# Keeping the two parts of mem in a DRAM scratch tensor between its four uses

## The chip, the cores and the metric

The kernel runs on one core of a Trainium2 chip. The metric is the device time of one execution in microseconds. The times quoted are medians of several runs; one further execution was recorded by the hardware profiler, and all rows of the trace come from it.

The engines appear under the names that the profile uses: PE (TensorE matmul), PEld (its weight loads), DVE (VectorE), ACT (ScalarE), POOL (GpSimd) and SP (SyncE, which issues most of the DMAs here).

## What is computed

A two-layer encoder trunk over 512 rows of width 1024. Each layer has a mixer, a cross-attention into `mem` (256 rows of width 1024, the same in both layers) and a gated MLP with a width-3 convolution; after each of the three the rows are normalised:

```python
for layer in range(DEPTH):                      # DEPTH = 2
    mix = mixer_ab(x, ...) if layer % 2 == 0 else mixer_c(x, ...)
    x = layer_norm(alpha * x + mix, ...)
    x = layer_norm(alpha * x + cross_attend(x, mem, wq, wkv, wo), ...)
    x = layer_norm(alpha * x + conv_ffn(x, w_up, conv_w, conv_b, w_down), ...)

def cross_attend(x, mem, wq, wkv, wo):
    kv = mem @ wkv                              # keys and values, 4 heads of 256
    probs = softmax(q @ k.T * 256 ** -0.5)
    return (probs @ v) @ wo
```

`mem` itself never changes, so the kernel reads the same 1 MB four times: for the keys and for the values of each layer.

## The kernel before

**Numbers in two parts.** Every fp32 operand x of a matmul is split into a high part h (x rounded to the fp32r type) and a low part l = x - h. `split` (lines 85 and 86) does it: a cast on ACT writes h, then a subtraction on DVE writes l. `mm3` (lines 223 to 225) makes a product of three matmuls: h h, h l, l h. In the trace a matmul row reads `ps<-moving,stationary`; weights are called `wh` and `wl`, activations `act`, accumulators in PSUM `ps`.

**Weights.** `plan` (from line 111) lists all weight tiles in the order of use. `Weights.load` keeps up to four of them loaded ahead: the DMA goes out on SP into one of 7 buffers `raw` (128x1024, 512 KB), and later `split` moves it into one of 5 pairs `wh`, `wl`. A `raw` buffer is free again when DVE has subtracted, a `wh` buffer when PE has used it. SP issues its DMAs in program order, so a DMA that has to wait for its buffer holds up all that follow.

**Activations.** 12 slots `act` of 128x2048 (h in the left half, l in the right). `mem`, turned so that its features lie on the partitions, takes two of them at each use: `load_mem` (line 639) calls `load_split` for each half, that is a 512 KB DMA into a `raw` buffer (line 90), a cast and a subtraction (128x1024 each).

**The four uses of mem.** First: loaded while the mixer's output projection of layer 0 runs, used by `proj_k` of layer 0. Second: loaded in `attend` of layer 0 after the queries, used by `proj_v` of layer 0. Third: loaded in the last down-projection of the MLP of layer 0, used by `proj_k` of layer 1. Fourth: loaded in the output projection of the mixer of layer 1, used by `proj_v` of layer 1. For the first, third and fourth the call comes through `ahead` from `load_ahead` (line 807).

**The fast product.** The third and fourth load stand in `fast_product` (lines 367 to 464), a product with seven block multiplications in place of eight. It goes through the weights in four passes. The passes use sums of weights that POOL makes: for each weight row of the second pass, lines 166 to 168 compute t3 (into a buffer `row`), t2 (in place, in the `raw` buffer of one weight, reading t3 and the second weight) and t4. So the second pass needs both weights of a row on chip before its first cast. The accumulators X and Y run on from the first pass into the second, and X into the third; between the passes DVE adds them to the rows x (line 379), and PE may go on in X only when DVE has read it. `ahead` is called inside the second pass.

**Order.** Each engine works through its own list in order. The order in the lists is made by a scheduler when the kernel is built, from the program order and estimated times, so leaving out instructions can also move others.

Of the kernel before, what the change touches and what calls it, by code (L numbers as in the profile page):

```python
# [8 lines left out]
F32 = mybir.dt.float32  # L9
# [5 lines left out]
P = 128  # L15
# [10 lines left out]
CH = 1024  # L26
# [10 lines left out]
def kernel(ctx: ExitStack, tc: tile.TileContext, a: dict, out: bass.AP):  # L37
    nc = tc.nc
# [8 lines left out]
    tpool = ctx.enter_context(tc.tile_pool(name="tpool", bufs=4))  # L47
    fpool = ctx.enter_context(tc.tile_pool(name="fpool", bufs=1))
    spool = ctx.enter_context(tc.tile_pool(name="spool", bufs=4))
    pspool = ctx.enter_context(tc.tile_pool(name="pspool", bufs=8, space=PSUM))  # L50

    uid = [0]

    def nm(s):
        uid[0] += 1
        return f"{s}{uid[0]}"
# [7 lines left out]
    def slot(dtype=F32R):  # L64

        return apool.tile([P, 2 * CH], dtype, tag="act", name=nm("act"))

    def duo(tag="act"):
        if tag == "act":
            t = slot()  # L70
            return t[:, :CH], t[:, CH:]
        h = wpool.tile([P, CH], F32R, tag="wh", name=nm("wh"))
        l = wpool.tile([P, CH], F32R, tag="wl", name=nm("wl"))
        return h, l

    def raw_tile():
        return rpool.tile([P, CH], F32, tag="raw", name=nm("raw"))
# [5 lines left out]
    def split(h, l, src):  # L83

        nc.scalar.copy(h, src)  # L85
        nc.vector.tensor_sub(l, src, h.bitcast(F32))  # L86

    def load_split(src, tag):
        raw = raw_tile()
        nc.sync.dma_start(raw, src)  # L90
        h, l = duo(tag)
        split(h, l, raw)
        return h, l
# [542 lines left out]
        return y  # L636


    def load_mem():
        return [load_split(a["memT"][i], "act") for i in range(2)]  # L640

    def mem_at(t, i, k, c):
        return t[k // 4][i][:, (k % 4) * MEM + c.start : (k % 4) * MEM + c.stop]
# [37 lines left out]
    def attend(layer, xT, kT, v):  # L681
# [55 lines left out]
        if v is None:  # L737
            for m in range(8):
                queries(m, m + 1)
            o, v, mem = Act(8), {}, load_mem()  # L740
            scores(0)
            v[0] = proj_v(layer, mem, 0)
            turn(0)
            scores(1)
            values(0)
            v[1] = proj_v(layer, mem, 1)
            turn(1)
            scores(2)
            values(1)
        else:  # L750
            for m in range(6):
                queries(m, m + 1)
            scores(0)
            queries(6, 7)
            scores(1)
            queries(7, 8)
            o = Act(8)
            turn(0)
            scores(2)
            turn(1)  # L760
            values(0)
            values(1)
# [39 lines left out]
        weights.load_beside(2 if k < 2 else 1, a["xT"][k], xT.tiles[k])  # L802
    weights.done(RING - 4)

    mem, left = [], None

    def load_ahead():
        mem.append(load_mem())

    for layer in range(2):  # L810
        if layer == 0:
            y = mixer_ab(xT)
            xT, left = residual_norm([(lambda: y, 0, 8)], "ab_w_out", "ln_mix", layer, ahead=load_ahead)
            kT = proj_k(layer, mem.pop(), {2: left[0]})
            v = None
        else:
            kT = proj_k(layer, mem.pop(), dict(zip((1, 2, 3), left)))
            y = mixer_c(xT)
            xT, left = residual_norm([(lambda: y, 0, 8)], "c_w_out", "ln_mix", layer, ahead=load_ahead)
            v = {0: proj_v(layer, mem[0], 0, {2: left[0]}), 1: proj_v(layer, mem.pop(), 1, {0: left[1], 5: left[2]})}  # L820
        o, hooks = attend(layer, xT, kT, v)
        xT, left = residual_norm([(lambda: o, 0, 8)], "xa_wo", "ln_xa", layer, hooks=hooks)
        up = [(lambda m0=m0, m1=m1, xT=xT, late=left[0]: ffn_up(layer, xT, late, m0, m1), m0, m1) for m0, m1 in FFN_GROUPS[layer]]
        xT, left = residual_norm(up, "ffn_w_down", "ln_ffn", layer, layer == 1, ahead=None if layer else load_ahead)
# [57 lines left out]
def build(shapes):  # L882
    import concourse.bacc as bacc

    nc = bacc.Bacc("TRN2", target_bir_lowering=False, num_devices=1)
    aps = {n: nc.dram_tensor(f"in_{n}", s, F32, kind="ExternalInput").ap() for n, s in shapes.items()}
    out = nc.dram_tensor("out_0_dram", (1, S, D), F32, kind="ExternalOutput").ap()
    with tile.TileContext(nc) as tc:
        kernel(tc, aps, out)
    return nc  # L890
# [9 lines left out]
```

## Time and profile before

| | us |
|---|---|
| Median of three runs | 1338.54 |
| The three runs | 1338.54, 1337.86, 1340.98 |
| The profiled execution | 1340.83 |
| Its span (first to last instruction) | 1339.1 |
| DVE busy | 880.7 |
| ACT busy | 511.2 |
| POOL busy | 190.3 |
| Mean granted clock of TensorE | 0.996 of full speed |

The profiled execution's time is 1.7 us longer than its span. "Busy" is the sum of the durations of an engine's instructions; issuing DMAs does not count. Matmuls are pipelined, with starts 0.23 us apart in a stream of 128x512 ones though each row is 0.39 us long, so time that PE loses is best seen in the distance between two starts. `[1.21 <-DVE wl L86]` behind a row is idle time of that engine just before it, and what ended it.

### The profile page before, as it was taken

The page shows a single profiled execution, that of the slowest core. Times are in us where ns is not written, and L with a number is a line of the kernel's source. Part 1 is how long each engine was busy: PE and PEld are TensorE (multiplying, and loading weights), DVE is VectorE, ACT ScalarE, POOL GpSimd, SP SyncE. Part 2 cuts the span into 40 slices and gives each one's busy share as a digit, 9 for nine tenths or more (in the row PEclk, how much of TensorE's full clock was granted, in tenths as well). Part 3 has the DMA queues.
Part 4 walks back from the last instruction along what each step waited for, and adds up shares of the span by engine and source line. Part 5 has one row for each costly group of instructions (what it writes and reads, how often), then busy time and mean ns, then how long its engine had stood idle before and what let it go on. Part 6 is the DMA issues. An engine that isn't in the chain of part 4 may idle for free.

```text
span 1339.1 us, 16258 instructions
## 1 busy us (share of the span) xinstructions
PE 1322.8 (99%) x6397; PEld 1113.0 (83%) x6397; DVE 880.7 (66%) x1135; ACT 511.2 (38%) x659; POOL 190.3 (14%) x160
## 2 busy tenths in 40 slices
PE   9999999999999999999999999999999999999996
PEld 7888888898888888887988887788898888888885
DVE  6668446576675676578945569936676685577446
ACT  5342344324343434343433334434144343343330
POOL 1002000010340220142100142100001320141001
PEclk9999999999999999999999999999999999999998
DMA  8633534223344344237433237531132353236301
GB/s 319 210 123 103 170 124 126 63 64 105 107 167 131 98 144 140 87 102 243 160 101 95 87 115 239 188 95 48 48 111 87 118 180 118 79 123 223 94 1 63
DMA packets 49469, 167.37 MB, mean 125 GB/s; under 512 B 5872, under 2 KB 6000, under 8 KB 49392
## 3 DMA queue, kind: packets, MB, share of 16 engines
q1 hardware_dynamic: 47664, 160.03, 36.9%
q0 software_dynamic: 1728, 6.29, 1.4%
q8 instruction: 50, 0.82, 0.2%
q14 instruction: 27, 0.22, 0.1%
HBM read 164.21 MB, written 2.10 MB: 124 GB/s over the span
## 4 chain that ended last, share of the span: by engine, by line
PE 92%; DVE 5%; issue 1%; DMA 1%; ACT 0%; POOL 0%; POOLq 0%; DVEq 0%; ACTq 0%
PE ps L223 30%; PE ps L224 30%; PE ps L225 30%; DVE wl L86 2%; PE ps L363 1%; DVE act L86 1%; DMA raw<-in_memT 1%; DVE x L338 1%; PE ps L724 1%; DVE stats L496 0%; DVE x L379 0%; POOL rs L335 0%; PE ps L798 0%; DVE x L336 0%; PE ps L598 0%
## 5 line engine op out<-in xcount | busy, mean ns | idle before, releaser
L86 DVE TENSOR_TENSOR wl<-raw,wh 128x1024 fp32r<-128x1024 f32 (+1 forms) x275 | 344.6, 1259 | 267.0 <-ACT wh L85 259.7
L85 ACT CAST wh<-raw 128x1024 fp32r<-128x1024 f32 (+1 forms) x275 | 286.5, 1042 | 540.1 <-PE ps L224 310.5
L223 PE MATMUL ps<-act,wh 128*128 128x512 f32 (+1 forms) x1284 | 472.6, 368 | 0.5 <-DVE act L86 0.5
L224 PE MATMUL ps<-act,wh 128*128 128x512 f32 (+1 forms) x1284 | 472.5, 368 | 0.0
L225 PE MATMUL ps<-act,wl 128*128 128x512 f32 (+1 forms) x1284 | 472.3, 368 | 0.0
L223 PEld LDWEIGHTS ps<-act,wh 128*128 128x128 f32 x1284 | 242.0, 189 | 41.1 <-DVE act L86 0.9
L224 PEld LDWEIGHTS ps<-act,wh 128*128 128x128 f32 x1284 | 242.1, 189 | 40.3 <-DVE act L86 0.3
L225 PEld LDWEIGHTS ps<-act,wl 128*128 128x128 f32 x1284 | 242.1, 189 | 40.2
L223 PE MATMUL ps<-wh,act 128*128 128x512 f32 (+1 forms) x664 | 259.6, 392 | 1.5 <-DVE x L379 1.5
L224 PE MATMUL ps<-wl,act 128*128 128x512 f32 (+1 forms) x664 | 258.7, 390 | 2.2 <-DVE wl L86 2.2
L225 PE MATMUL ps<-wh,act 128*128 128x512 f32 (+1 forms) x664 | 258.1, 389 | 0.0
L224 PEld LDWEIGHTS ps<-wl,act 128*128 128x128 f32 x664 | 125.2, 189 | 29.6 <-DVE wl L86 4.6
L223 PEld LDWEIGHTS ps<-wh,act 128*128 128x128 f32 x664 | 125.6, 189 | 28.8 <-DVE x L379 3.1
L225 PEld LDWEIGHTS ps<-wh,act 128*128 128x128 f32 x664 | 125.2, 189 | 25.6
L335 POOL TENSOR_TENSOR rs<-rs,mhalf 128x1 f32<-128x1 f32 x28 | 41.0, 1468 | 535.4 <-DVE rs L334 508.5
L159 POOL TENSOR_TENSOR raw<-raw,raw 128x512 f32<-128x512 f32 x23 | 32.6, 1415 | 449.7 <-DVE wl L86 375.1
L85 ACT CAST act<-ps 128x512 fp32r<-128x512 f32 x104 | 56.8, 591 | 71.1 <-PE ps L363 51.9
L86 DVE TENSOR_TENSOR act<-ps,act 128x512 fp32r<-128x512 f32 x104 | 67.5, 683 | 10.9 <-ACT act L85 10.8
L379 DVE SCALAR_TENSOR_TENSOR x<-x,ps 128x512 f32<-128x512 f32 x96 | 61.6, 679 | 9.8 <-PE ps L225 9.8
L86 DVE TENSOR_TENSOR act<-blocks,act 128x768 fp32r<-128x768 f32 (+1 forms) x46 | 61.5, 1349 | 8.5 <-ACT act L85 8.5
L625 DVE SCALAR_TENSOR_TENSOR tmp<-ps,convw,tmp 128x511 f32<-128x511 f32 x88 | 65.6, 745 | 1.6
L784 DVE TENSOR_TENSOR blocks<-tmp,ps 128x512 f32<-128x512 f32 x38 | 26.1, 687 | 59.8 <-PE ps L225 57.6
(80 smaller groups left out, 810.1 us busy)
## 6 DMA issues: line engine op xcount, KB each, us to landing
raw<-in_ffn_w_up SPq DMA_DIRECT2D x88, 512.0 KB, 3.6
raw<-in_ffn_w_down SPq DMA_DIRECT2D x63, 512.0 KB, 3.6
raw<-in_c_w_in SPq DMA_DIRECT2D x24, 512.0 KB, 3.6
raw<-in_xa_wk SPq DMA_DIRECT2D x16, 512.0 KB, 3.9
raw<-in_xa_wq SPq DMA_DIRECT2D x16, 512.0 KB, 4.1
raw<-in_xa_wv SPq DMA_DIRECT2D x16, 512.0 KB, 3.6
raw<-in_xa_wo SPq DMA_DIRECT2D x16, 512.0 KB, 4.2
raw<-in_c_w_out SPq DMA_DIRECT2D x12, 512.0 KB, 3.6
```

The costliest lines, as they stand in the source:

```text
L85: nc.scalar.copy(h, src)
L86: nc.vector.tensor_sub(l, src, h.bitcast(F32))
L159: nc.gpsimd.tensor_sub(both("t1"), w1[:, half[0]], w0[:, half[0]])
L223: nc.tensor.matmul(ps, lh, rh, start=start, stop=False, skip_group_check=more)
L224: nc.tensor.matmul(ps, lh, rl, start=False, stop=False, skip_group_check=more)
L225: nc.tensor.matmul(ps, ll, rh, start=False, stop=stop, skip_group_check=more)
L335: nc.gpsimd.tensor_tensor(rs, rs, mhalf, op=ALU.pow)
L338: nc.vector.scalar_tensor_tensor(z[:, c], z[:, c], rs[:, 0:1], b[:, c], op0=ALU.mult, op1=ALU.add)
L363: nc.tensor.transpose(ps[:, k * P : (k + 1) * P], xt[t][:, (half * 4 + k) * P : (half * 4 + k + 1) * P], ident)
L379: return nc.vector.scalar_tensor_tensor(z, z, scale, ps, op0=ALU.mult, op1=ALU.add)
L625: nc.vector.scalar_tensor_tensor(dst[:, s:], src[:, : S - s], tap(2 - s), dst[:, s:], op0=ALU.mult, op1=ALU.add)
L784: hid.put(m, lambda to: nc.vector.tensor_mul(to, *(v.rearrange("p (i s) -> p i s", i=2) for v in (g, ps[2 * i + 1]))))
```

## The change

A pool in DRAM with two tensors `mem0` and `mem1` (128x2048, 1 MB each) is added. The first call of `load_mem` does what it did, and stores each slot, h and l side by side, to its tensor. The other three calls load the slots from these tensors: one 1 MB DMA for each half, no `raw` buffer, no cast and no subtraction. All of these DMAs are issued on SP.

```diff
+    dpool = ctx.enter_context(tc.tile_pool(name="dpool", bufs=1, space=bass.MemoryType.DRAM))
...
-    def load_mem():
-        return [load_split(a["memT"][i], "act") for i in range(2)]
+    memory = [dpool.tile([P, 2 * CH], F32, tag=f"mem{i}", name=f"mem{i}") for i in range(2)]
+
+    def load_mem(first=False):
+
+        tiles = []
+        for i in range(2):
+            t = slot()
+            tiles.append((t[:, :CH], t[:, CH:]))
+            if first:
+                raw = raw_tile()
+                nc.sync.dma_start(raw, a["memT"][i])
+                split(*tiles[i], raw)
+                nc.sync.dma_start(memory[i], t.bitcast(F32))
+            else:
+                nc.sync.dma_start(t.bitcast(F32), memory[i])
+        return tiles
...
-    mem, left = [], None
+    mem, left, first = [], None, [False, False, True]
 
     def load_ahead():
-        mem.append(load_mem())
+        mem.append(load_mem(first.pop()))
```

Lines of the kernel after the change stand one lower up to line 639, and buffers have other numbers: what is `x_113` to `x_116` before is `x_115` to `x_118` after. The accumulators X, Y of the product named below are `ps_4779`, `ps_4780` (X) and `ps_4781`, `ps_4782` (Y) in both.

**SP at the third use** (end of the last down-projection of layer 0). Before:

```order
L147 DMA raw_4834<-in_ffn_w_down 128x1024
L147 DMA raw_4836<-in_ffn_w_down 128x1024
L90 DMA raw_4919<-in_memT 128x1024
L90 DMA raw_4924<-in_memT 128x1024
L183 DMA raw_4929<-in_xa_wk 128x1024
L183 DMA raw_4947<-in_xa_wk 128x1024
```

After:

```order
L148 DMA raw_4834<-in_ffn_w_down 128x1024
L654 DMA act_4919<-mem_119 128x2048
L148 DMA raw_4836<-in_ffn_w_down 128x1024
L654 DMA act_4921<-mem_120 128x2048
L184 DMA raw_4923<-in_xa_wk 128x1024
L184 DMA raw_4941<-in_xa_wk 128x1024
```

The first load of mem has moved ahead of `raw_4836`, the second weight that POOL needs for the last row of the second pass, and is twice as large. The fourth use has the same pattern with `in_c_w_out`.

**DVE at the third use**, between the second and the third pass. `wl_4932` and `wl_4950` are weights of the third and the fourth pass, `wl_4968` the last of the fourth. Before:

```order
L496 BN_STATS stats_4776<-x_114 128x6
L86 TENSOR_TENSOR act_4921<-raw_4919,act_4921 128x1024
L86 TENSOR_TENSOR act_4926<-raw_4924,act_4926 128x1024
L86 TENSOR_TENSOR wl_4932<-row_4807,wh_4931 128x1024
L86 TENSOR_TENSOR wl_4950<-raw_4718,wh_4949 128x1024
L86 TENSOR_TENSOR wl_4968<-raw_4810,wh_4967 128x1024
L379 SCALAR_TENSOR_TENSOR x_113<-x_113,ps_4779 128x512
L379 SCALAR_TENSOR_TENSOR x_114<-x_114,ps_4780 128x512
```

After (`wl_4926`, `wl_4944` and `wl_4962` are the same three weights):

```order
L497 BN_STATS stats_4776<-x_116 128x6
L87 TENSOR_TENSOR wl_4926<-row_4807,wh_4925 128x1024
L87 TENSOR_TENSOR wl_4944<-raw_4718,wh_4943 128x1024
L380 SCALAR_TENSOR_TENSOR x_115<-x_115,ps_4779 128x512
L87 TENSOR_TENSOR wl_4962<-raw_4810,wh_4961 128x1024
L380 SCALAR_TENSOR_TENSOR x_116<-x_116,ps_4780 128x512
```

The two subtractions of mem are gone, and the addition from the first accumulator stands ahead of the last weight's subtraction.

**PE at the third use**, from the end of the second pass. Before:

```order
L225 MATMUL ps_4782<-wh_4893,act_4772 128x512
L223 MATMUL ps_4905<-wh_4949,act_4309 128x512
L224 MATMUL ps_4905<-wl_4950,act_4309 128x512
L225 MATMUL ps_4905<-wh_4949,act_4309 128x512
L223 MATMUL ps_4906<-wh_4949,act_4309 128x512
L223 MATMUL ps_4779<-wh_4897,act_4309 128x512
L224 MATMUL ps_4779<-wl_4898,act_4309 128x512
```

After:

```order
L226 MATMUL ps_4782<-wh_4893,act_4772 128x512
L224 MATMUL ps_4779<-wh_4897,act_4309 128x512
L225 MATMUL ps_4779<-wl_4898,act_4309 128x512
L226 MATMUL ps_4779<-wh_4897,act_4309 128x512
L224 MATMUL ps_4780<-wh_4897,act_4309 128x512
```

Four matmuls of the fourth pass (into `ps_4905` and `ps_4906`) stood ahead of the third pass and now follow it, so that the third pass, with `ps_4779`, comes directly behind the second. The fourth use has both of these shifts too.

At the first use each store to `mem0`, `mem1` stands on SP behind the subtraction of its half, with four and two of the loads of `xa_wk` of layer 0 after them. At the second use the two loads stand behind the first two loads of `xa_wo` instead of ahead of them.

## The prediction

> **What bounds the kernel now.** I read the page's busy line first, then PE's waits, then the two stretches in which PE waits, there the chain and the timelines.
>
> The busy line of the page:
>
> ```profile
> PE 1322.8 (99%) x6397; PEld 1113.0 (83%) x6397; DVE 880.7 (66%) x1135; ACT 511.2 (38%) x659; POOL 190.3 (14%) x160
> ```
>
> PE is busy for 1322.8 of 1339.1 us. Work taken off DVE and ACT can therefore be worth only what PE waits for them. All of PE's waits but one at the start (engine, line, awaited: total us, times, longest):
>
> ```profile
> PE ps L224 <- DVE wl L86: 2.2, 2, 1.2
> PE ps L223 <- DVE x L379: 1.5, 2, 0.8
> PE ps L363 <- DVE act L86: 0.7, 1, 0.7
> PE ps L223 <- DVE act L86: 0.5, 2, 0.3
> ```
>
> That is 4.9 us, all on DVE. The windows view (length, then busy us of PE, PEld, DVE, ACT, POOL, granted clock, DMA share, GB/s) shows where:
>
> ```profile
> 621.00:629.00 8.00, 6.01 (x18) 4.17 (x18) 7.56 (x11) 1.04 (x1) 0.53 (x1) 0.79 0.98 342
> 629.00:665.00 36.00, 35.25 (x261) 33.28 (x261) 34.74 (x47) 17.97 (x24) 6.09 (x4) 1.00 0.47 153
> 821.00:826.00 5.00, 3.22 (x13) 2.06 (x12) 5.00 (x6) 1.04 (x1) 0.53 (x1) 1.00 0.86 265
> 826.00:865.00 39.00, 38.49 (x184) 31.24 (x182) 38.44 (x53) 18.98 (x24) 8.29 (x6) 1.00 0.60 208
> ```
>
> Place A is 621 to 629 (third use of mem), place B 821 to 826 (fourth). Both are the last quarter of a fast product, and DVE is nearly full there and after. At A the clock is 0.79 over 8 us, that is 0.21 x 8 = 1.7 us of PE time lost, beside the waits. The first and second use (near 90 and 190 us) lie in stretches without a wait.
>
> The chain of work at A (start, us, what):
>
> ```profile
> 605.68 5.57 DMA raw<-in_memT
> ...
> 612.23 1.05 ACT wh L85
> ...
> 613.31 0.99 DVE wl L86
> ...
> 618.06 1.86 DVE act L86 x2
> ...
> 620.24 3.49 DVE wl L86 x3
> 623.73 0.61 DVE x L379
> ```
>
> So mem is in it twice: ACT, in order, stands before the two casts of mem until its load lands, and the weight cast behind them starts at 612.23; then the two splits on DVE (the 1.86 of the chain) stand ahead of the weight splits and of the addition that PE waits for. PE and DVE there:
>
> ```profile
> 621.05 0.39 PE L223 MATMUL ps<-wh,act 128*128 128x512 f32 x1
> 622.65 0.50 PE L224 MATMUL ps<-wl,act 128*128 128x512 f32 x1 [1.21 <-DVE wl L86]
> 622.99 0.40 PE L225 MATMUL ps<-wh,act 128*128 128x512 f32 x1
> 623.22 0.39 PE L223 MATMUL ps<-wh,act 128*128 128x512 f32 x1
> 624.38 0.58 PE L223 MATMUL ps<-wh,act 128*128 128x512 f32 x1 [0.77 <-DVE x L379]
> ```
>
> ```profile
> 617.98 2.35 DVE L86 TENSOR_TENSOR act<-raw,act 128x1024 fp32r<-128x1024 f32 x2
> ```
>
> From 622.99 to 623.22 the pitch of a matmul is 0.23. Against it the steps 621.05 to 622.65, 622.65 to 622.99 and 623.22 to 624.38 are 1.37 + 0.11 + 0.93 = 2.4 us too long. **A costs 2.4 + 1.7 = 4.1 us.** At B:
>
> ```profile
> 821.68 0.39 PE L223 MATMUL ps<-wh,act 128*128 128x512 f32 x1
> 823.07 0.50 PE L224 MATMUL ps<-wl,act 128*128 128x512 f32 x1 [1.01 <-DVE wl L86]
> 823.41 0.40 PE L225 MATMUL ps<-wh,act 128*128 128x512 f32 x1
> 823.65 0.39 PE L223 MATMUL ps<-wh,act 128*128 128x512 f32 x1
> 824.81 0.50 PE L223 MATMUL ps<-wh,act 128*128 128x512 f32 x1 [0.77 <-DVE x L379]
> ```
>
> 1.16 + 0.11 + 0.93 = **2.2 us at B**, at full clock.
>
> **The change part by part.** *Removed:* six casts on ACT and six splits on DVE, two at each later use. Those at the second use are worth nothing (no wait of PE near it). At A and B the two splits free 2.26 us of DVE (617.98 to 620.24), and the orders show that the additions from the first two accumulators now stand before or between the weight splits, and that PE no longer puts four products of the last weight ahead.
>
> *Place A worked through.* The big load goes onto SP's queue between the two last down-projection weights. Those two, the two loads of mem that now follow them, and the DMA traffic:
>
> ```profile
> L147 SPq DMA_DIRECT2D raw<-in_ffn_w_down x2: 327/327/327, 602.3 to 603.4; - x2
> ...
> DMA to landing us min/median/max: 3.5/4.2/4.9
> ```
>
> ```profile
> L90 SPq DMA_DIRECT2D raw<-in_memT x2: 328/328/328, 604.6 to 605.7; - x2
> ...
> DMA to landing us min/median/max: 5.4/5.5/5.6
> ```
>
> ```profile
> 608.00:610.00 2.00, 2.00 (x11) 1.65 (x10) 2.00 (x4) 0.02 (x1) 1.52 (x1) 1.00 0.90 367
> ```
>
> The first lands at 605.8, the second at 603.4 + 4.9 = 608.3. A megabyte at 367 GB/s takes 2.9 us, half a megabyte 1.4. With the big load ahead of it the second weight lands at 605.8 + 2.9 + 1.4 = 610.1, **1.8 us later**. POOL and ACT behind it:
>
> ```profile
> 608.42 1.52 POOL L167 TENSOR_TENSOR raw<-row,raw 128x512 f32<-128x512 f32 x1 [1.20 <-DMA raw<-in_ffn_w_down]
> ```
>
> ```profile
> 615.80 1.06 ACT L85 CAST wh<-raw 128x1024 fp32r<-128x1024 f32 x1 [0.63 <-PE ps L225]
> 618.57 1.05 ACT L85 CAST wh<-raw 128x1024 fp32r<-128x1024 f32 x1 [1.71 <-PE ps L225]
> ```
>
> L167 then runs 610.1 to 611.5. The cast that stood behind mem (612.23) can start at 611.5 and ends at 612.5, its split on DVE at 613.7 (a split takes 1.13 of DVE, an addition or a statistic 0.6), the first row weight's at 614.8, two additions and two statistics at 617.2, the second row weight's at 618.3, the next weight's at 619.5 (its cast, the 615.80 one, is long done), the addition from the first accumulator at 620.1, the last weight's split at 621.3 (cast 618.57), the addition from the second accumulator at 621.9. PE needs the first at 621.05 and the second three matmuls later, at 621.7. So the wait left is 0.2 us, and with it goes the half clock. **A gives 4.1 - 0.2 = 3.9.** What is late next is that second addition.
>
> *Place B:* the same order, with the two last weights of that product here:
>
> ```profile
> L147 SPq DMA_DIRECT2D raw<-in_c_w_out x2: 328/328/328, 801.0 to 804.1; - x2
> ```
>
> The second goes out 3.1 us after the first, so the big load is through before it: at most 0.6 us later. The wait left is 0.1: **2.1.**
>
> *The waits behind A and B* (36.00 - 35.25 = 0.75 and 39.00 - 38.49 = 0.51) are on transposes of normalised rows, with DVE full. At A DVE saves 2.26 of work, 0.8 by the earlier cast, and up to 1.3 of idle time that I put down to PE's slow stretch (34.74 of 36.00 busy): 4.3 against PE's 3.9. The wait stays or shrinks: 0.1. At B 2.26 + 0.8, the same earlier cast assumed, is 3.1 against 2.1: I take all of the 0.51. Together 0.6, with bounds of -1.0 (DVE does not follow) and +1.3.
>
> *Added at the first use:* two stores, each behind its split in SP's order, with the weights for the keys behind them. Second split of mem, and the next weight cast that needs a load from there:
>
> ```profile
> 96.26 1.22 DVE L86 TENSOR_TENSOR act<-raw,act 128x1024 fp32r<-128x1024 f32 x1
> ...
> 118.06 1.05 ACT L85 CAST wh<-raw 128x1024 fp32r<-128x1024 f32 x1 [4.83 <-PE ps L225]
> ```
>
> The last store waits until 97.5, the loads behind it land before 110, which is 8 us ahead of that cast: cost 0, and without that margin whatever passes 118. No store of this size is in the trace. Bounds: 0 and, as four of the slowest loads in a row (4 x 5.6 = 22 us from 97.5), 2 us. I take 0.
>
> *Second use:* the loads now stand behind two weights:
>
> ```profile
> L90 SPq DMA_DIRECT2D raw<-in_memT x2: 327/328/328, 177.1 to 182.6; - x2
> ```
>
> ```profile
> 194.01 0.40 PE L223 MATMUL ps<-wh,act 128*128 128x512 f32 x1
> ```
>
> Those weights take the two raw buffers and times of mem (177.1, 182.6); the first big load goes out at 183.0 and lands near 183 + 3.6 + 2.9 = 189.5, the first product of it is at 194.0. Cost 0, 4.5 us of cover; a load that took 11.2 us (two of 5.6) would land at 194.2: cost 0.2 at most.
>
> **Sum**, against the profiled execution (1340.83 us, span 1339.1): 3.9 + 2.1 + 0.6 = 6.6, so 1334.2. That execution stands 2.3 above the median of 1338.54, and the half-clock stretch may be its own: without it the gain is 4.9 and the median gives 1333.6. Between them, **1333.8 us**.
>
> [...]
>
> **The rivals.**
>
> *DVE takes the gain back at the transposes.* For it: 34.74 of 36.00 and 38.44 of 39.00 busy. Then A gives only what DVE saves itself, 2.26 + 0.8 = 3.1 of the profiled 4.1, less the 1.7 of clock where a run has none of it, and B 2.1 with no 0.6: about 3.4 off the median, 1335.1. Against it: the 1.3 of idle time. Chance 0.22.
>
> *The big load holds up the weights.* If a megabyte takes 5.6 us of the queue and not 2.9, the weight at A lands at 612.8, the whole chain above moves by 2.7, PE waits 1.75 for the first addition and 1.1 for the second: A's waits are as long as now, and B keeps 1.5: 1337.0. For it: DMA share 0.90 there. Against it: 367 GB/s. Chance 0.16. [...]
>
> *Slower.* The same mechanism past its point: from a landing of 613 on, each further us at A is a us of PE, beside the half clock. At 11.2 us a megabyte (two loads of 5.6 in a row) the weight lands at 618.4 and PE waits some 8 us at A for the 4.1 there now, as well as at B: up to 1348; halfway 1343. Chance 0.05.
>
> *The half clock was in every timed run:* 1338.54 - 6.6 = 1331.9. For it: the third timed run is 1340.98. Chance 0.12. *The reloading does not take place* (flag taken from the wrong end): the list ends in True, so the first load splits and three reload; 0.01, 1338.5.
>
> **How the numbers follow.** Forecast 0.44, at 1333.6 to 1334.2. A change of 0.3% (4.0 us, below 1334.5) is about what can be told from none. Faster: 0.12, nearly all of 0.44, a little of the first rival: 0.57. Same: the rest of the first two rivals and the last: 0.38. Slower 0.05. The range, 1331.5 to 1337.5, takes in the bounds of the waits behind A and B and most of the second rival.
>
> **What would show it.** PE's waits on DVE wl and x at A and B gone or under 0.3 us; clock 1.00 at A; POOL L167 starting near 610 there; no split act<-raw on DVE after 100 us. Wrong, if POOL L167 starts after 612.5, if PE waits more for transposes than the 0.75 and 0.51 now, or if PE waits near 194 us.

## The result and the profile after

The changed kernel takes **1332.08 us** (median of 4 runs, 1331.86 to 1332.91), the kernel before 1338.2 us beside it: ratio 0.995, 95% interval 0.9938 to 0.9962. The profiled execution took 1331.86 us with a span of 1330.1, 9.0 us less than the span before. The kernel before spreads more than the changed one: 1337.37 to 1345.07 in 18 later runs.

The busy line of the changed kernel, and all of PE's waits (engine, line, awaited: total us, times, longest). The helpers stand one line further down, so L223 of before is L224 here.

```profile
PE 1318.7 (99%) x6397; PEld 1111.3 (84%) x6397; DVE 873.0 (66%) x1129; ACT 505.9 (38%) x653; POOL 188.7 (14%) x160
```

```profile
PE ps L813 <- DVE zeros L810: 1.2, 1, 1.2
PE ps L225 <- DVE wl L87: 0.2, 1, 0.2
```

Of the 4.9 us of waits on DVE 0.2 is left, and that lies near 384 us, at neither place. The windows that answer to those of before (length, busy us of PE, PEld, DVE, ACT, POOL, granted clock, DMA share, GB/s):

```profile
617.00:625.00 8.00, 8.00 (x37) 6.47 (x36) 6.92 (x10) 3.16 (x3) 0.53 (x1) 1.00 0.87 279
625.00:661.00 36.00, 36.00 (x266) 34.11 (x265) 35.76 (x49) 17.41 (x23) 6.09 (x4) 1.00 0.48 159
809.00:817.00 8.00, 8.00 (x37) 6.46 (x36) 7.54 (x11) 3.01 (x4) 1.13 (x2) 1.00 0.89 341
817.00:856.00 39.00, 38.97 (x187) 32.10 (x187) 38.46 (x53) 19.62 (x25) 8.30 (x6) 1.00 0.59 197
```

PE has no idle time at A and behind it and 0.03 us behind B, the clock at A is 1.00 instead of 0.79 (half, 0.50, from 625 to 628 in the profile of before), and DVE is still nearly full behind both places (35.76 of 36.00, 38.46 of 39.00).

Where the 9.0 us came from is read from five matmuls that both programs run at the same point: one well ahead of A, one ahead of and one behind the transposes that follow A, one behind B, and one behind the waits that follow B. Before:

```profile
402.36 0.45 PE L223 MATMUL ps<-wh,act 128*128 128x512 f32 x1
649.28 0.36 PE L223 MATMUL ps<-act,wh 128*128 128x256 f32 x1
658.00 0.39 PE L223 MATMUL ps<-act,wh 128*128 128x256 f32 x1
847.47 0.48 PE L223 MATMUL ps<-wh,act 128*128 128x512 f32 x1
911.94 0.36 PE L223 MATMUL ps<-act,act 128*128 128x256 f32 x1
```

And after:

```profile
402.25 0.46 PE L224 MATMUL ps<-wh,act 128*128 128x512 f32 x1
644.88 0.36 PE L224 MATMUL ps<-act,wh 128*128 128x256 f32 x1
652.65 0.39 PE L224 MATMUL ps<-act,wh 128*128 128x256 f32 x1
839.86 0.48 PE L224 MATMUL ps<-wh,act 128*128 128x512 f32 x1
903.38 0.36 PE L224 MATMUL ps<-act,act 128*128 128x256 f32 x1
```

The lead is 0.11, 4.40, 5.35, 7.61 and 8.56 us. So A gave 4.3 (1.7 of it the half clock), the transposes behind A 0.95, B 2.26, the products behind B 0.95, and all the rest 0.5.

### The profile page after: what moved, and what is told of

It reads as the page before. It is cut to its first block, busy times and chain, and to the rows that moved or that the text cites. A ratio compares the mean times of both kernels' runs of the same rounds, so it can differ in the third digit from the quotient of the medians.

```text
span 1330.1 us, 16252 instructions
## 1 busy us (share of the span) xinstructions
PE 1318.7 (99%) x6397; PEld 1111.3 (84%) x6397; DVE 873.0 (66%) x1129; ACT 505.9 (38%) x653; POOL 188.7 (14%) x160
## 4 chain that ended last, share of the span: by engine, by line
PE 97%; DVE 1%; issue 1%; DMA 0%; POOL 0%; POOLq 0%; SPq 0%; DVEq 0%; ACT 0%
PE ps L225 32%; PE ps L224 32%; PE ps L226 32%; PE ps L364 1%; PE ps L739 1%; DMA raw<-in_ab_w_v 0%; POOL rs L336 0%; DVE x L339 0%; PE ps L599 0%; DVE wl L87 0%; DVE stats L497 0%; DVE act L87 0%; DVE x L489 0%; DVE blocks L275 0%; POOLq L903 0%
## 5 line engine op out<-in xcount | busy, mean ns | idle before, releaser
L87 DVE TENSOR_TENSOR wl<-raw,wh 128x1024 fp32r<-128x1024 f32 (+1 forms) x275 | 341.1, 1245 | 263.9 <-ACT wh L86 256.4
L224 PE MATMUL ps<-act,wh 128*128 128x512 f32 (+1 forms) x1284 | 472.2, 368 | 0.0
L224 PEld LDWEIGHTS ps<-act,wh 128*128 128x128 f32 x1284 | 242.0, 189 | 40.3 <-issue 0.3
L224 PE MATMUL ps<-wh,act 128*128 128x512 f32 (+1 forms) x664 | 258.1, 389 | 0.0
L224 PEld LDWEIGHTS ps<-wh,act 128*128 128x128 f32 x664 | 124.6, 188 | 26.6 <-DVE x L380 1.1
```

The lines of the kernel that those rows point to most:

```text
L224: nc.tensor.matmul(ps, lh, rh, start=start, stop=False, skip_group_check=more)
```

## The experiments

Each kernel computes the whole result. The first group is written against the changed kernel, whose `load_mem` has a mode there instead of the flag: "store" (split the input and store the parts), "split" (as before the change), "load" (from the scratch tensor) and three more that are shown where they are used.

**Which use gives what.** One kernel takes the second use back, one keeps the reload at the third use alone, one at the fourth alone, and one only stores.

```diff
 # second_split
-            o, v, mem = Act(8), {}, load_mem()
+            o, v, mem = Act(8), {}, load_mem("split")
 # only_third (the list is read from its end; the second use splits as well)
+    modes = ["split", "load", "store"]
 # only_fourth
+    modes = ["load", "split", "store"]
 # store_alone
+    modes = ["split", "split", "store"]
```

> The second use of mem casts and splits it from the input again, as the kernel before does; the first use splits and stores, the third and fourth load from the scratch tensor. It computes the whole result. Theory (the gain comes from the third use, A, and the fourth, B, alone): 1332.1 us, within 0.5, and no wait of PE near 190 us. Rival (the second use helps too, because its raw buffers or its place on SP come free for other weights): 1333 us or more, and loads or casts between 180 and 200 us that end later than in the changed kernel.

> Only the third use (A) loads the parts; the second and fourth split as before, the first splits and stores. It computes the whole result. Theory: PE's waits at A and on the transposes behind it go (2.4 + 0.75 = 3.2 us without the half-clock stretch, 4.9 with it), those at B stay at 2.2 and 0.5: 1335.0 us when the stretch is not in the timed runs, 1333.3 when it is. Rival (DVE is full behind A and gives the gain back at the transposes): 1336 us or more, with more than 0.75 us of waits on the transposes behind A.

> Only the fourth use (B) loads the parts; the second and third split as before, the first splits and stores. It computes the whole result. Theory: the waits at B (2.2 us) and on the transposes behind it (0.5 to 1.0) go, those at A stay: 1335.0 to 1335.5 us, and the gains of this kernel and of the one with only the third use add up to the 6.1 us of the whole change. Rival (DVE gives it back at the transposes behind B): 1336.2 us or more. If the half-clock stretch at A is in the timed runs, this kernel keeps it and stands 4.9 us above the changed one, at 1337.

> The first use splits and stores both halves; the other three uses split again as before and nothing reads the scratch tensor. It computes the whole result. Theory: the stores cost nothing, 1338.2 us within 0.5, with PE's waits at A and B as before (2.2 us on wl and 1.5 on x together). Rival (the stores or their places on SP hold up the weights of the keys): up to 1340.2 us, with a wait of PE before 130 us.

Measured beside 1339.07 us for the kernel before: second use split 1332.03 (ratio 0.9945, interval 0.9933 to 0.9958), third alone 1334.98 (0.9967, 0.9955 to 0.998), fourth alone 1335.47 (0.9973, 0.9962 to 0.9983), stores alone 1339.21 (0.9996, 0.9985 to 1.0007). The second use and the stores are worth nothing that can be measured. The two gains, 4.1 and 3.6, add up to 7.7, beside 7.0 for both in the same runs and 6.1 in the first. In the windows of the kernel with the third use alone, A is full and B still waits:

```profile
617.00:625.00 8.00, 8.00 (x37) 6.46 (x36) 7.89 (x12) 2.91 (x3) 0.53 (x1) 1.00 0.97 337
817.00:825.00 8.00, 5.96 (x26) 4.25 (x25) 8.00 (x12) 2.10 (x2) 0.53 (x1) 1.00 0.92 320
```

**Half of the split at a time.** At A and B one half of each part is loaded, the other made from the input as before.

```diff
 # keep_sub: the high half is loaded, ACT's cast is gone
+    nc.sync.dma_start(tiles[i][0].bitcast(F32), memory[i][:, :CH])
+    nc.vector.tensor_sub(tiles[i][1], raw, tiles[i][0].bitcast(F32))
 # keep_cast: the low half is loaded, DVE's subtraction is gone
+    nc.sync.dma_start(tiles[i][1].bitcast(F32), memory[i][:, CH:])
+    nc.scalar.copy(tiles[i][0], raw)
```

> At A and B the high half is loaded from the scratch tensor, and the low half is made on DVE by the subtraction from the input, as before; only the casts on ACT are gone. Second use loads. It computes the whole result. Theory (the two subtractions on DVE, ahead of the additions that PE waits for, are what costs): 2.26 us of DVE come back at each place; about 1.0 of it fits in DVE's idle time there, so PE waits 1.3 at each place and a little behind it: 1334.7 to 1335.5 us. Rival (the casts on ACT, in order behind the landing of mem, are what costs): 1332.1 to 1332.6 us, no wait at A or B.

> At A and B the low half is loaded from the scratch tensor, and the high half is cast on ACT from the input, as before; only the subtractions on DVE are gone. Second use loads. It computes the whole result. Theory (DVE's subtractions are what costs, the casts delay the next weight cast by 0.8 us only): 1332.1 to 1332.9 us, waits at A and B together under 0.8 us. Rival (the casts on ACT are what costs): 1335 to 1337.5 us, with waits on wl at A and B near 1 us each.

Both missed what either theory gave: keep_sub 1348.68 us beside 1338.86 (1.0068, 1.0054 to 1.0082), slower than before by 9 to 10, and keep_cast 1339.27 (0.9998, 0.9986 to 1.0009; its runs lie between 1335.92 and 1342.2). The first of keep_sub's subtractions on DVE, and the matmul that then waits at A (idle time ahead of a row and what ended it in brackets):

```profile
611.16 1.23 DVE L655 TENSOR_TENSOR act<-raw,act 128x1024 fp32r<-128x1024 f32 x1 [5.10 <-DMA raw<-in_memT]
```

```profile
615.34 0.76 PE L224 MATMUL ps<-wh,act 128*128 128x512 f32 x1 [4.62 <-DVE x L380]
```

The scheduler had put the subtraction early on DVE, ahead of a weight split. The two loaded halves go ahead of the inputs on SP, 2 MB with them, and DVE, in order, stood 5.1 us before a load. In keep_cast the same happens to ACT, where the last row is the weight cast:

```profile
610.91 1.05 ACT L659 CAST act<-raw 128x1024 fp32r<-128x1024 f32 x1 [3.38 <-DMA raw<-in_memT]
612.16 1.05 ACT L659 CAST act<-raw 128x1024 fp32r<-128x1024 f32 x1 [0.20 <-DMA raw<-in_memT]
613.12 1.04 ACT L86 CAST wh<-raw 128x1024 fp32r<-128x1024 f32 x1
```

That cast is at 609.69 in the changed kernel. So these two tested the landing of the input more than the work. What they show is the price of an engine that stands, in its order, before a load that has not landed: 5.1 and 3.38 us here.

**More bytes.** Each reload is issued twice.

```diff
+            elif mode == "twice":
+                for _ in range(2):
+                    nc.sync.dma_start(t.bitcast(F32), memory[i])
```

> At A and B each half of mem is loaded from the scratch tensor twice into the same buffer; the second copies stand behind the first on SP and wait for these to land, with the weights of the next product behind them (2 MB more at each place). Second use loads once. It computes the whole result. Theory (the reloads have some 9 us of room: the first weight behind them lands near 612 and its cast is at 621): that weight lands near 618.5, so 1332.1 to 1333 us and no wait at A or B over 0.5 us. Rival (the queue is the bound there, and transfers that come later stop PE): 1335 us or more, PE waiting for weights behind A and B.

Measured 1333.05 us (0.995, 0.9938 to 0.9963), as the theory had it. SP's queue at A shows the first weight of the next product some 8 us later than in the changed kernel (604.24):

```profile
612.81 11.32 SPq L184 DMA_DIRECT2D raw<-in_xa_wk  x8
```

Two more megabytes at each place cost about 1 us in all. They stand behind the weights that A itself waits for, and PE has no wait at A or B. How much could be put ahead of those was not tried.

**The clock.** The kernel before once more, for another profile.

> The kernel before, unchanged, for another profile of it. Theory: the waits of PE at A and B come back at 2.2 and 1.5 us in total, but the half-clock stretch at A is a matter of the single execution: an execution of about 1338.2 us shows a clock of 1.00 there, and A then loses 2.4 us and not 4.1. Rival (the stretch belongs to A's waits): a clock near 0.79 in the 8 us at A again.

It took 1339.04 us (1.0, 0.9992 to 1.0009). Its profiled execution, and that of the kernel with the stores alone, in the 8 us at A and at B:

```profile
620.60:628.60 8.00, 6.12 (x20) 4.25 (x19) 7.95 (x11) 1.04 (x1) 0.53 (x1) 0.79 0.85 316
820.80:828.80 8.00, 6.17 (x26) 4.47 (x25) 8.00 (x10) 1.90 (x2) 0.53 (x1) 1.00 0.85 312
```

```profile
617.00:625.00 8.00, 7.02 (x30) 5.18 (x29) 8.00 (x9) 2.10 (x2) 0.53 (x1) 1.00 0.81 264
818.00:826.00 8.00, 6.20 (x20) 4.33 (x19) 8.00 (x11) 1.04 (x1) 0.53 (x1) 0.79 0.90 316
```

The stretch is at A in one and at B in the other, always behind waits, and in the profiles of the kernels with the third or the fourth use alone it is at neither, though one place still waits. By itself the second profile of before fits the rival, the other three do not: the stretch belongs to the waits but comes only in some executions. Among all the profiles of this study it is in 7 of the 11 whose kernels wait by more than 0.3 us at A, at B or behind them, and in none of the three whose kernels don't. The mean granted clock of each timed run says the same. Of the 85 runs of the kernel before that stand beside the experiments, 32 show 0.996 or less, with a median of 1340.3 us, and 53 show 0.997 or more, with a median of 1338.3; all four of the changed kernel show 0.997 or 0.998. By that sign the stretch is in about a third of the executions of before, which take some 1.9 us longer, and the change gains 6.2 us where it is absent.

**The casts or the subtractions elsewhere.** In the kernel before, the casts of mem at A and B move from ACT to POOL, or the subtractions from DVE to POOL.

```diff
 # cast_pool
+    nc.gpsimd.tensor_copy(h, raw)
 # sub_pool
+    nc.gpsimd.tensor_sub(l, raw, h.bitcast(F32))
```

> The kernel before, with the two casts of mem at the third and the fourth use moved from ACT to POOL; every other engine's order is that of the kernel before, and every use loads and splits the input. It computes the whole result. Theory formed after the runs with half of the split: the loss at A is the sum of two delays less some 2 us of room that DVE has there, 2.2 us by which ACT's casts, in order behind the landing of mem, hold up the next weight cast (612.23 against about 610), and 2.26 us of DVE's subtractions. With the first gone, the room covers the second: weight cast near 610, waits at A and B together under 1.2 us, 1333.5 to 1335 us. Rival (the recorded one: DVE's subtractions are the cost, the cast delay is worth 0.8 us a place): 1337 us or more. Rival (only ACT's delay costs): 1332 us and no wait at A and B.

> The kernel before, with the two subtractions of mem at the third and the fourth use moved from DVE to POOL; the casts of mem stay on ACT in the same place, and every use loads and splits the input. It computes the whole result. Theory of the two delays: the weight cast stays near 612.2, DVE is 2.26 us ahead behind it and its room covers the rest: waits at A and B together under 1.2 us, 1333.5 to 1335 us. Rival (DVE's subtractions are all of the cost): 1332 us, no wait. Rival (only ACT's delay costs): 1337 us or more, waits at A and B as before.

Measured beside 1338.78: cast_pool 1337.45 us (0.9989, 0.998 to 0.9997), the rival's figure for DVE's subtractions as the cost, though one weight split beside POOL's casts took 2.05 us. The other, sub_pool, 1339.93 (1.0009, 0.9998 to 1.002), lies in the open range of the last rival (1337 or more) but without its waits: PE waits 1.92 and 0.70 us at A, both for additions, and none for a weight. POOL and DVE there:

```profile
608.54 2.17 POOL L168 TENSOR_TENSOR raw<-raw,raw 128x512 f32<-128x512 f32 x1
610.66 5.75 POOL L648 TENSOR_TENSOR act<-raw,act 128x1024 fp32r<-128x1024 f32 x2
```

```profile
609.47 1.87 DVE L379 SCALAR_TENSOR_TENSOR x<-x,ps 128x512 f32<-128x512 f32 x3
612.04 2.11 DVE L86 TENSOR_TENSOR wl<-raw,wh 128x1024 fp32r<-128x1024 f32 x1 [0.71 <-ACT wh L85]
614.07 3.41 DVE L86 TENSOR_TENSOR wl<-row,wh 128x1024 fp32r<-128x1024 f32 x1
```

A weight split takes 1.22 us alone. Beside POOL's work two of them took 2.11 and 3.41, 3.1 us more, and the move had saved 2.26. The runs on POOL therefore don't separate the two delays.

**The same work at another place.** Last, in the kernel before, the subtractions are queued behind the second addition, and in a second kernel the casts also behind the last weight cast of that product. Nothing leaves its engine and nothing is stored.

```diff
 # both kernels, behind done_after(added, 1) of the fast product
+            with tc.issue_after(added.ins):
+                nc.vector.tensor_sub(l, raw, h.bitcast(F32))
 # both_behind, ahead of it
+            with tc.issue_after(casts[-1].ins):
+                nc.scalar.copy(h, raw)
```

`casts` lists the casts of `split` on ACT, in the order in which the program issues them.

> The kernel before with one thing moved: at the third and fourth use the two subtractions of mem on DVE are queued behind the second addition that PE waits for; the casts of mem stay on ACT where they were, and no scratch tensor is used. It computes the whole result. Theory of the two delays (ACT's casts hold the weight cast by some 2.2 us, DVE's subtractions take 2.26 us, and DVE is full up to the transposes behind): idle time of PE in the 8 us at A falls from 2.0 to 0 to 0.6 us, but DVE has the same work ahead of the transposes and still starts it late, so most of it comes back there (over 1.3 us behind A): 1336.5 to 1338.2 us. Rival (the place of the subtractions ahead of the additions is the whole cost): about 1333 to 1334 us.

> As the kernel that queues only the subtractions behind, and the two casts of mem on ACT are also queued behind the last weight cast of that product, so that no cast of mem stands ahead of a weight cast there. No scratch tensor; it computes the whole result. Theory of the two delays: the weight cast runs near 610 again, idle time at A 0, and DVE is 2.2 us earlier at the transposes than with the subtractions moved alone, which leaves 0 to 1 us of waits behind A and as much behind B: 1333 to 1335 us, at least 2 us below the other. Rival (the cast on ACT is worth little, 0.8 us a place or less): within 1.6 us of the other kernel. Rival (the room is enough without any scratch tensor): 1332 us, the same as the change.

Measured beside 1339.33: sub_behind 1339.0 us (1.0001, 0.9992 to 1.001), both_behind 1338.55 (0.9993, 0.9984 to 1.0002). In the first PE idles 0.14 us at A, as the theory of the two delays has it, and the time is 0.8 us above its range. The second missed that theory by 3.5 us, and agrees with the rival by which the cast is worth little. Its timed runs show a mean clock of 0.996 or less more often than those of before beside it (8 of 11, 8 of 21), so the medians hide a part of its gain. An addition shortly before A that waits for PE serves as the zero of each run's clock. In both_behind, that one and the first of the two additions at A, then PE at the transposes behind A and the first matmul after them:

```profile
606.62 0.69 DVE L381 SCALAR_TENSOR_TENSOR x<-x,ps 128x512 f32<-128x512 f32 x1 [1.31 <-PE ps L227]
618.86 0.69 DVE L381 SCALAR_TENSOR_TENSOR x<-x,ps 128x512 f32<-128x512 f32 x1 [1.00 <-PE ps L227]
```

```profile
653.75 1.16 PE L365 MATMUL ps<-ident,x 128*128 128x128 f32 x8 [2.04 <-DVE act L88]
654.86 0.39 PE L225 MATMUL ps<-act,wh 128*128 128x256 f32 x1
```

The zero and the same matmul in sub_behind, and the zero of the kernel before:

```profile
606.63 0.69 DVE L381 SCALAR_TENSOR_TENSOR x<-x,ps 128x512 f32<-128x512 f32 x1 [1.29 <-PE ps L227]
```

```profile
655.02 0.39 PE L225 MATMUL ps<-act,wh 128*128 128x256 f32 x1
```

```profile
606.97 0.69 DVE L379 SCALAR_TENSOR_TENSOR x<-x,ps 128x512 f32<-128x512 f32 x1 [1.31 <-PE ps L225]
```

And in the changed kernel the zero and the two additions at A:

```profile
606.64 0.69 DVE L380 SCALAR_TENSOR_TENSOR x<-x,ps 128x512 f32<-128x512 f32 x1 [1.29 <-PE ps L226]
618.88 0.69 DVE L380 SCALAR_TENSOR_TENSOR x<-x,ps 128x512 f32<-128x512 f32 x1 [0.98 <-PE ps L226]
620.63 1.28 DVE L380 SCALAR_TENSOR_TENSOR x<-x,ps 128x512 f32<-128x512 f32 x2
```

At A the two are alike, and DVE even idles 1.0 us for PE ahead of the first addition. But behind A DVE is full (35.76 of 36.00 us in the changed kernel), so 2.26 us more of it make PE wait 2.04 us at the transposes. From the zero to the first matmul behind them it is 46.01 us in the changed kernel and 48.24 in both_behind: 2.23 more, DVE's two subtractions to within 0.03. With the subtractions alone moved it is 48.39, so the cast of mem ahead of the weight cast adds 0.15 there. In the kernel before, where mem landed later, it is 51.03 (to 658.00), or 49.3 without the 1.7 of half clock: 1.1 on top of the 2.23. Two more profiles have the old order and full clock at A: 48.44 with the stores alone, 49.90 with the fourth use alone. In these four kernels the weight cast behind mem starts 4.26 us after the zero (stores alone), 4.58 (sub_behind), 5.20 (fourth use alone) and 5.26 (before), so the long ones are those with the late cast.

B gives the same. From an addition ahead of B (802.26 in the changed kernel, 804.50 in both_behind, 804.60 in sub_behind, 807.60 before) to the fifth of the products that follow the transposes there (854.05, 858.52, 859.28, 862.60) it is 51.79, 54.02, 54.68 and 55.00 us. Up to 0.3 in the two middle ones is half clock, which begins at 858 to 859 there (starts 0.43 us apart instead of 0.23).

## Why the prediction was right, and where it was not

*Where and why.* The waits at A and B went, the clock at A came back, no split of mem stands on DVE after 100 us, and no wait came near 194 us: as predicted, and by the reason given. DVE's 2.26 us at each place are the larger part of what PE pays for. The last pair shows it: they cost some 2.2 of 3.3 us at A (the clock aside) and 2.0 to 2.2 of 3.2 at B, even when queued behind the additions. For ACT's order the prediction had 0.8; sub_behind beside both_behind gives 0.15 at A and 0.6 to 0.7 at B. What else makes up the remaining 1.1 us of before (up to 1.7 in the kernel with the fourth use alone) goes with a late weight cast, but was not separated by a run.

*Place A, 3.9 forecast, 4.3 measured.* The sum is right. One step of it, the big load making the second weight 1.8 us later, is hardly to be seen in the profile of the changed kernel, but it is in others. The row of POOL and the cast that the prediction followed:

```profile
608.36 1.30 POOL L168 TENSOR_TENSOR raw<-row,raw 128x512 f32<-128x512 f32 x1 [1.86 <-DMA raw<-in_ffn_w_down]
```

```profile
609.69 1.05 ACT L86 CAST wh<-raw 128x1024 fp32r<-128x1024 f32 x1 [2.63 <-DVE x L380]
```

SP's queue ahead of them, and two windows of the traffic:

```profile
600.89 0.33 SPq L148 DMA_DIRECT2D raw<-in_ffn_w_down  x1
601.27 0.42 SPq L654 DMA_DIRECT2D act<-mem  x1
603.11 0.33 SPq L148 DMA_DIRECT2D raw<-in_ffn_w_down  x1
```

```profile
606.00:608.00 2.00, 2.00 (x10) 1.69 (x9) 1.36 (x2) 1.05 (x1) 0.50 (x1) 1.00 1.01 414
608.00:610.00 2.00, 2.00 (x10) 1.65 (x9) 2.00 (x4) 0.31 (x1) 1.56 (x2) 1.00 1.00 422
```

The zero addition is 0.33 earlier in this run, so 608.36 is 608.7 by the clock of before, where 608.4 stood and 610.1 was expected: 0.3 later and not 1.8. The first weight and the big load were issued 1.1 us earlier than the weights of before (600.89 and 601.27 beside 602.3), and the DMA engines moved 414 to 422 GB/s where the sum took 367. Where the issue was not early, the delay is there. The kernel with the second use split has the same order at A and issued these two at 601.96 and 602.34; its zero and POOL's row:

```profile
606.58 0.69 DVE L380 SCALAR_TENSOR_TENSOR x<-x,ps 128x512 f32<-128x512 f32 x1 [1.30 <-PE ps L226]
609.44 1.29 POOL L168 TENSOR_TENSOR raw<-row,raw 128x512 f32<-128x512 f32 x1 [2.58 <-DMA raw<-in_ffn_w_down]
```

That is 609.8 by the clock of before, 1.4 later, and the kernels with the third use alone and with the reloads issued twice give 1.3 and 1.4. So the delay was near what the prediction said, and the 0.3 belongs to an execution that issued the loads early. The start of this row scatters in any case: over the profiles of this study it lies 0.5 to 2.0 us behind the zero where nothing is loaded between the two weights, and 1.7 to 2.9 where 1 MB is. PE waits at A in none of the four kernels with the order of the changed one. The additions ran 0.2 to 0.3 us ahead of the forecast with the weight early and with it late, and the 0.2 of wait that was expected is not there.

*Place B, 2.1 forecast, 2.26 measured.* The number is right, but the weight was not at most 0.6 us later. POOL's row with the second weight starts 0.34 us behind the addition at 807.60 before (807.94), and 2.24 behind the one at 802.26 in the changed kernel (804.50): 1.9 later. That can't be put down to the big load alone, as both_behind, without it, has 1.80 (806.30). It cost nothing, so there was more room than the working had.

*Behind A and B, 0.6 forecast, 1.9 measured.* This is the mis-sized term, and it passed its own bound of +1.3. The prediction took the idle time of PE in the two windows, 0.75 and 0.51, as all that could be had there, and of it 0.1 at A. At A the larger part was missed. The prediction counted a lead of 4.3 for DVE against 3.9 for PE, and took 0.1 of the difference. The split of the transposed rows, which the transposes there wait for, before and after:

```profile
656.06 3.08 DVE L86 TENSOR_TENSOR act<-ps,act 128x512 fp32r<-128x512 f32 x5
```

```profile
650.72 1.88 DVE L87 TENSOR_TENSOR act<-ps,act 128x512 fp32r<-128x512 f32 x3
```

DVE leads by 5.34 there and PE by 4.40 ahead of the transposes: 0.94, the 0.95 that came. At B its own count of DVE's lead, 3.1 against 2.1 for PE, gave the 1.0 that came; the cap was wrong. What waits behind B are not transposes but products of the split rows, and two rows of before show what the cap missed:

```profile
861.40 0.49 PE L223 MATMUL ps<-act,wh 128*128 128x512 f32 x1 [0.28 <-DVE act L86]
862.09 0.47 PE L223 MATMUL ps<-act,wh 128*128 128x512 f32 x1 [0.20 <-DVE act L86]
```

The step between them is 0.69 us at a pitch of 0.23, so 0.46 is lost, and only 0.20 of it is called idle: the row of the matmul before, 0.49 long, covers the rest.

*The sum.* Profile to profile 6.6 was forecast and 9.0 measured: 1.3 of the difference is that term, 0.6 are A and B, 0.5 lies elsewhere. In medians 1338.54 to 1333.8 was forecast, and 1332.08 came. Without the half clock the traces give 2.6 at A, 0.95, 2.26 and 0.95, that is 6.8, beside 6.2 by the timed runs of before that are without it.

*The rivals.* That DVE takes the gain back at the transposes is what happens to a change that moves work, not to this one, which removes it: both_behind waits 2.04 us there, the changed kernel not at all. The half clock in every timed run gave the nearest figure, 1331.9, but for a wrong reason, since it comes only in some executions (7 of the 11 profiles with waits). The big load does go with a later weight, but not to 612.8 or 618.4, as the two rivals on it had: the latest POOL L168 at A is 610.04, with the reloads issued twice, and PE does not wait. The stores and the second use cost nothing, as forecast.

## What to carry to other kernels

Where PE waits at several places behind one another and the awaited engine is full between them, count that engine's work over the whole stretch: moving work from the first wait carried it to the next here (2.04 us at the transposes in both_behind), while removing it shortened both (2.6 and 0.95 us at A and behind it). For the size of a wait take the steps between starts less the pitch, not the idle time of a window: behind B 0.46 us was lost where 0.20 was called idle. Before a cast or a split is queued, ask whether its input has landed by its turn: in keep_sub DVE stood 5.1 us before a load, and PE waited 4.62 us for the addition behind it.

## What the runs showed of the hardware

In sub_pool two weight splits on DVE (`wl<-raw,wh` and `wl<-row,wh`), beside POOL's subtractions of mem, took 2.11 and 3.41 us, against 1.22 each in the profile of before (613.31 and 614.45), where POOL does nothing from 611.3 to 616. The three additions at 609.47, which read an accumulator (`x<-x,ps`), ran beside POOL's work in 1.87, the 0.6 apiece that two take without it (1.28 at 620.63 in the changed kernel). Why the splits slow down and the additions do not was not tested.

The half clock lasts about 3.4 us in the profile of before: 0.21 of 8 us is lost, and the granted clock is 0.66 from 624.5 to 625, 0.50 from 625 to 628 and 0.93 from 628 to 628.5. Matmuls there start 0.43 us apart instead of 0.23. It comes behind waits of about 1.2 and 0.8 us, or of 1.6 behind B in both_behind, in some executions at A, in some at B, in some not at all. What sets it off was not shown.

A reload of 1 MB into SBUF, and a store of the same size, in the changed kernel, by the view of DMA issues (KB each, median us from issue to landing):

```profile
act<-mem SPq DMA_DIRECT2D x6, 1024.0 KB, 6.5
mem<-act SPq DMA_DIRECT2D x2, 1024.0 KB, 6.1
```
